# Rows of the first expert by one-hot products on chip, and one looped body for overfull experts

## Chip, cores and metric

One core of one Trainium2 chip runs the whole kernel. The metric is device time in microseconds (us), from launch to end, median over runs. The profile is one execution of its own; the times of its rows count from its first instruction.

## What is computed

A decoder block over 512 tokens of 1024 channels: a token mixer, a layer norm, a mixture of 16 experts (each token goes to 2 of the 4 experts of its best group), and a second layer norm. The change lies at the entry of the mixture.

```python
h = layer_norm(DEEPNORM_ALPHA * h + mix, ln1_g[l], ln1_b[l])
...
group_logits = (t @ router_group_w + router_group_b).astype(f32)
group_p, group_idx = lax.top_k(jax.nn.softmax(group_logits, axis=-1), 1)
...
exp_p, exp_idx = lax.top_k(jax.nn.softmax(in_group, axis=-1), TOP_K_IN_GROUP)
...
h = jax.nn.silu(jnp.einsum("td,edf->tef", t, expert_w_gate)) \
    * jnp.einsum("td,edf->tef", t, expert_w_up)
h = h * combine[:, :, None].astype(h.dtype)
y = jnp.einsum("tef,efd->td", h, expert_w_down)
```

## The kernel before

Tokens lie in four tiles of 128 (`NT` = 4) in `HT`. All large products are three passes on split operands: a high part (written by ScalarE) and a low part (raw minus high, by VectorE); L805 and L809 make the two parts of a piece of expert weights, L1183 and L1184 those of an expert's transposed rows, and L1203, L1204, L1205 multiply high by high, high by low and low by high.

The end of the mixer and the router are one hand-written list of steps (a string, L990 on): `c` and `e` are output projections, `t` transposes, `l` logits, `f` the layer norm of a token tile, `g` the choice of experts, `r` the ranks of the tile's tokens within their experts, and `w8` eight products of ones that use no data (L224). TensorE keeps that order. `choose` writes one-hot rows of the two chosen experts (`EO`, `EA`); `ranks` multiplies `EA` with a triangle (L977), picks each token's rank (L979), and `rank_one_hot` (L929) writes `RO`, a 128 x 128 one-hot matrix of token against rank, for each of a token's two choices.

Behind the list `rank_tokens` (L1024) multiplies `RO` with token numbers, so that column e of `idx` (L1026) lists the 128 rows of expert e. L1034 and L1036 find the largest count, which the program then loads as a branch condition (L1073, L1076): if an expert has more than `CAP` = 128 tokens, a long body treats the others. `gather(e)` (L1042) fetches the rows of expert e from `hD`, a copy of `HT` in device memory (stored at L951), by an indirect DMA that GpSimd issues, into one of five buffers `XG`. The gates (L1054 to L1067) run on VectorE with two exponentials on ScalarE (L1056, L1062); all this stands ahead of the branch. Behind the branch come the low parts of expert 0's weights, tables for the gates and slots (L1137 to L1160), then `turn(0)`: eight transposes of expert 0's rows (L1181) and their two parts, and `gate_up(0, 0)`, its first products. `K` keeps instructions in the order of the program on their engine; the other instructions are put in place by a scheduler. Each engine works through its own list in order.

Of the kernel before, what the change touches and what calls it, by code (L numbers as in the profile page):

```python
# [19 lines left out]
D = 1024  # L20
S = 512
NT = 4
# [14 lines left out]
def body(ctx: ExitStack, tc: tile.TileContext, P: dict, out):  # L37
# [832 lines left out]

    rt = temps(48, 54)
    jp2 = rt(128, dt=I32)
# [19 lines left out]
    EO, EA, rk2 = cst(NT, 2, 16), cst(NT, 16, dt=BF16), cst(NT, 2)  # L892
    TE = late(NT, 2, 2, 16, dt=BF16)
    cmp, ra, rb_, oh2, s16 = rt(5, 4, 4), rt(5, 4), rt(5, 4), rt(2, 5, 4), rt(16)

# [77 lines left out]
    def ranks(i):  # L973

        p = pb()
        for m in range(i + 1):
            K(T.matmul(p[:, 0:16], upper_s if m == i else ones_b, EA[:, m], start=m == 0, stop=m == i))  # L977
        for n in range(2):
            V.scalar_tensor_tensor(s16, EO[:, i, n], 1.0, p[:, 0:16], op0=ALU.mult, op1=ALU.mult,  # L979
                                   accum_out=rk2[:, i, n:n + 1])  # L980
        rank_one_hot(RO, rk2, i)

        V.tensor_scalar(TE[:, i, :, 0], EO[:, i], float(128 * i), None, op0=ALU.mult)
        V.tensor_scalar(TE[:, i, :, 1], EO[:, i], pid, None, op0=ALU.mult)


# [4 lines left out]
    for step in """c0a t00 t10 t01 c0b l00 l10 l01 t11 t20 t30 c1a l11 l20 l30 t02 t03 t21 t31 c1b l02 l03 l21 l31 c2a f0 g0 t12  # L991
                   t13 c2b l12 l13 r0 e0a f1 g1 t22 t23 e0b l22 l23 r1 e1a f2 t32 e1b g2 l32 r2
                   t33 l33 f3 g3 w8 r3""".split():
        kind, v = step[0], [int(x) for x in step[1:3] if x.isdigit()]
        if kind == "c":
            out_half(1, v[0], int(step[2] == "b"))
        elif kind == "e":
            out_half(1, NT - 1, int(step[2] == "b"), slice(v[0] * 256, v[0] * 256 + 256))
        else:
            {"t": transposes, "l": logits_part, "f": finish, "g": choose, "r": ranks, "w": warm}[kind](*v)  # L1000
    eload()
# [14 lines left out]
    rke = cst(NE - NL, NT)  # L1016
    rkv = rke.rearrange("p e i -> p i e")

    def rank_tokens(dst, ro):
# [17 lines left out]

    XG = [reg(o, D) for o in (184, 188, 192, 0, 4)]

    def gather(e):  # L1040
# [4 lines left out]
    earlier = esplit(0, True)  # L1045
    gather(0)
    second = gather(1)
# [22 lines left out]
    yO = dram.tile([(NBLK - 1) * NE * CAP, D], F32, name="yO")  # L1070
    iD = dram.tile([NE * (NBLK - 1), CAP, 1], I32, name="iD")
    with tc.issue_after(second.ins):
# [3 lines left out]
    with tc.If(most > CAP):  # L1076
        OW, OX, OXT, OY = reg(40, 2048), reg(192, D), reg(48, KT, 128), reg(192, D)
        OS, OFT = reg(52, FF), reg(53, FF)
        ORO = reg(48, NT, 2, 128, dt=BF16)
        oidx, ork, oi = cst(NBLK - 1, 16, dt=I32), cst(NT, 2), cst(1, dt=I32)  # L1080
        V.tensor_scalar(gto, rk2, float(CAP), None, op0=ALU.is_ge)
        V.tensor_tensor(gto, gt, gto, ALU.mult)
        for b in range(1, NBLK):
            V.tensor_scalar(ork, rk2, float(CAP * b), None, op0=ALU.subtract)
            for i in range(NT):
                rank_one_hot(ORO, ork, i)
            rank_tokens(oidx[:, b - 1], ORO)
            SP.dma_start(iD.rearrange("(e b) p o -> p b (e o)", b=NBLK - 1)[:, b - 1], oidx[:, b - 1])
        with tc.For_i(0, NE, 1) as eo:
            wex = lambda nm, r: P[nm][0][bass.ds(eo, 1)].rearrange("o (k p) f -> p (o k) f", p=128)[:, r]  # L1090
            for b in range(1, NBLK):
                SP.dma_start(oi, iD[bass.ds(eo * (NBLK - 1) + (b - 1), 1)].rearrange("b p o -> p (b o)"))
                G.indirect_dma_start(out=OX, out_offset=None, in_=hD,
# [23 lines left out]
                for n in range(2):  # L1117
# [4 lines left out]
                    V.tensor_copy(OY[:, ns], p)  # L1122
                SP.dma_start(yO[bass.ds(eo * ((NBLK - 1) * CAP) + (b - 1) * CAP, CAP)], OY)
        osl, oslf = cst(NT, 2, dt=I32), cst(NT, 2)
# [305 lines left out]
```

## Time and profile before

| | |
|---|---|
| three runs | 828.6, 829.49, 836.26 us, median 829.49 |
| profiled execution, its own time | 829.64 us |
| its span, first to last instruction | 827.9 us |
| busy: TensorE, VectorE, ScalarE, GpSimd | 94%, 65%, 46%, 13% |
| mean granted clock of TensorE | 0.976 |

A row of a timeline gives start and busy time of an instruction (or of a run of like ones, xN), engine, line, operation, output <- inputs, and in brackets how long the engine was idle before it and what ended that. PE is TensorE, DVE VectorE, ACT ScalarE, POOL GpSimd; a q behind the name is the engine's sequencer. PEclk is the granted clock of TensorE, 1.00 being 2.4 GHz and 0.50 being 1.2 GHz.

### The profile page before, as it was taken

What the parts mean: (1) busy time and instruction counts of PE and PEld (TensorE: products, weight loads), DVE (VectorE), ACT (ScalarE), POOL (GpSimd) and SP (SyncE); (2) the same over time, 40 slices, a digit from 0 to 9 for tenths busy, and PEclk for the clock granted to TensorE, in tenths of its full rate; (3) what the DMA queues carried; (4) which work ended last, traced back from release to release, by engine and by line L of the source; (5) the groups of instructions that cost most, each with busy time, mean ns of one, the idle gap of its engine ahead of it and who ended that gap; (6) DMA issues with size and microseconds to landing.
All of it is one profiled execution on the core that took longest, in us unless ns stands there. A gap on an engine that the chain in (4) does not pass through costs nothing.

```text
span 827.9 us, 10853 instructions
## 1 busy us (share of the span) xinstructions
PE 779.1 (94%) x4043; PEld 647.5 (78%) x4043; DVE 535.5 (65%) x1026; ACT 385.0 (46%) x612; POOL 106.7 (13%) x90
## 2 busy tenths in 40 slices
PE   8879999999999999999999999999994999999991
PEld 7567888787889988888788888888773788888780
DVE  3337882997575992547633332323578899999987
ACT  2485353453335542423322222222323899899843
POOL 0002002001100000000500000001031202110177
PEclk9998999999999999999999999999996999999996
DMA  9526336336260135343244333369818899999762
GB/s 225 87 59 169 79 81 143 84 69 154 46 139 2 51 72 95 94 102 77 99 129 103 103 101 103 102 241 331 291 52 260 297 382 388 367 341 307 280 250 101
DMA packets 110752, 133.65 MB, mean 161 GB/s; under 512 B 19780, under 2 KB 93032, under 8 KB 110696
## 3 DMA queue, kind: packets, MB, share of 16 engines
q1 hardware_dynamic: 107240, 120.33, 50.2%
q0 software_dynamic: 3456, 12.58, 4.3%
q8 instruction: 33, 0.54, 0.3%
q14 instruction: 23, 0.19, 0.1%
HBM read 120.82 MB, written 12.08 MB: 161 GB/s over the span
## 4 chain that ended last, share of the span: by engine, by line
PE 76%; issue 9%; DVE 9%; DMA 2%; ACT 2%; POOL 1%; POOLq 0%; DVEq 0%; SPq 0%; ACTq 0%
PE pa L237 16%; PE pa L236 16%; PE pa L235 16%; PE pa L1205 5%; PE pa L1203 4%; PE pa L1204 4%; PE pb L1181 2%; PE pb L525 1%; DVE r L809 1%; DVE r L386 1%; PE pb L607 1%; PE pb L592 1%; PE pb L509 1%; DMA r<-hD,r 1%; PE pb L414 1%
## 5 line engine op out<-in xcount | busy, mean ns | idle before, releaser
L235 PE MATMUL pa<-r,r 128*128 128x512 f32 (+1 forms) x712 | 280.1, 393 | 7.5 <-ACT r L149 7.3
L236 PE MATMUL pa<-r,r 128*128 128x512 f32 (+1 forms) x712 | 278.3, 391 | 2.2 <-DVE r L150 2.2
L237 PE MATMUL pa<-r,r 128*128 128x512 f32 (+1 forms) x712 | 277.5, 390 | 0.0
L150 DVE TENSOR_TENSOR r<-r,r 128x2048 fp32r<-128x2048 f32 (+2 forms) x48 | 102.8, 2148 | 134.6 <-ACT r L149 134.6
L235 PEld LDWEIGHTS pa<-r,r 128*128 128x128 f32 x712 | 134.4, 189 | 35.6 <-ACT r L149 8.1
L236 PEld LDWEIGHTS pa<-r,r 128*128 128x128 f32 x712 | 134.5, 189 | 29.5 <-DVE r L150 3.2
L237 PEld LDWEIGHTS pa<-r,r 128*128 128x128 f32 x712 | 134.3, 189 | 27.3 <-DVE r L232 0.4
L149 ACT ACTIVATE r<-r 128x2048 fp32r<-128x2048 f32 (+2 forms) x48 | 84.8, 1777 | 143.3 <-PE pa L236 82.0
L809 DVE TENSOR_TENSOR r<-r,r 128x1024 fp32r<-128x1024 f32 x96 | 117.1, 1222 | 5.6 <-ACT r L805 3.9
L805 ACT ACTIVATE r<-r 128x1024 fp32r<-128x1024 f32 x96 | 96.3, 1059 | 0.0
L1203 PE MATMUL pa<-r,r 128*128 128x512 f32 x192 | 78.2, 407 | 0.0
L1205 PE MATMUL pa<-r,r 128*128 128x512 f32 x192 | 75.9, 395 | 1.0 <-DVE r L1305 1.0
L1204 PE MATMUL pa<-r,r 128*128 128x512 f32 x192 | 75.6, 394 | 0.0
L386 DVE SCALAR_TENSOR_TENSOR r<-pa,r,r 128x511 f32<-128x511 f32 (+2 forms) x72 | 53.5, 743 | 15.7 <-ACT r L384 15.2
L1205 PEld LDWEIGHTS pa<-r,r 128*128 128x128 f32 x192 | 36.0, 188 | 9.9 <-DVE r L1305 1.9
L1203 PEld LDWEIGHTS pa<-r,r 128*128 128x128 f32 x192 | 36.3, 189 | 7.1 <-ACT r L1183 0.2
L1204 PEld LDWEIGHTS pa<-r,r 128*128 128x128 f32 x192 | 36.3, 189 | 6.9
L387 ACT ACTIVATE r<-r 128x512 f32<-128x512 f32 x24 | 15.1, 630 | 46.7 <-DVE r L386 42.9
L1042 POOL DMA_INDIRECT r<-hD,r x16 | 21.1, 1317 | 91.4 <-PE pb L1181 37.3
L758 POOL TENSOR_TENSOR r<-r,r 128x512 f32<-128x512 f32 x8 | 10.3, 1290 | 146.2 <-DVE r L757 142.0
L384 ACT ACTIVATE r<-pa,r 128x512 f32<-128x512 f32 x24 | 16.3, 680 | 25.2 <-PE pa L237 25.2
L1181 PE MATMUL pb<-r,r 128*128 128x128 f32 x128 | 20.2, 284 | 8.3 <-DMA r<-hD,r 8.2
(325 smaller groups left out, 899.0 us busy)
## 6 DMA issues: line engine op xcount, KB each, us to landing
r<-in_w_in_dram SPq DMA_DIRECT2D x29, 1024.0 KB, 8.9
r<-in_expert_w_gate_dram SPq DMA_DIRECT2D x32, 512.0 KB, 6.8
r<-in_expert_w_down_dram SPq DMA_DIRECT2D x16, 1024.0 KB, 8.4
r<-in_expert_w_up_dram SPq DMA_DIRECT2D x32, 512.0 KB, 8.4
yD<-r SPq DMA_DIRECT2D x12, 512.0 KB, 9.7
r<-in_x_dram SPq DMA_DIRECT2D x8, 512.0 KB, 5.9
r<-in_w_dn_out_dram SPq DMA_DIRECT2D x4, 1024.0 KB, 5.5
r<-in_w_sgu_out_dram SPq DMA_DIRECT2D x4, 1024.0 KB, 6.0
```

The source lines that it names most:

```text
L149: pin(A.activation(hi, raw, AF.Copy))
L150: pin(eng.tensor_tensor(lo, raw, f_(hi), ALU.subtract))
L235: pin(T.matmul(o, lh, rh, start=first, stop=False))
L236: pin(T.matmul(o, lh, rl, start=False, stop=False))
L237: pin(T.matmul(o, ll, rh, start=False, stop=last))
L386: V.scalar_tensor_tensor(acc[:, s:], p[:, :S - s], wc(3 - s), acc[:, s:], op0=ALU.mult, op1=ALU.add)
L805: K(A.activation(hi[:, s], raw[:, s], AF.Copy))
L809: K(V.tensor_tensor(lo[:, s], raw[:, s], f_(hi[:, s]), ALU.subtract))
L1181: K(T.transpose(p[:, u * 128:(u + 1) * 128], XG[e % 5][:, k * 128:(k + 1) * 128], ident))
L1203: K(T.matmul(args[0], args[1], args[3], start=args[5], stop=False))
L1204: K(T.matmul(args[0], args[1], args[4], start=False, stop=False))
L1205: K(T.matmul(args[0], args[2], args[3], start=False, stop=args[6]))
```

## The change

Expert 0's rows are no longer gathered. For each token tile VectorE makes `OH0`, a float matrix of token against rank that is one where the token is expert 0's (two instructions, L984 and L985 of the changed kernel). A new step `d` multiplies it with the tile of `HT` (L997, two products of 128 x 512, summed over the four tiles in two PSUM banks); d0 to d2 take the place of `w8`, d3 stands behind r3. ScalarE copies one half of the sum to `XG[0]` (L1033), VectorE the other (L1034). `gather(0)` goes. The code for overfull experts becomes one body in nested loops over blocks and experts instead of three copies; its index table is laid out by block.

```diff
-    rt = temps(48, 54)
+    rt = temps(48, 52)
...
+    OH0 = reg(52, NT, 128)
...
         rank_one_hot(RO, rk2, i)
 
+        V.tensor_scalar(OH0[:, i], RO[:, i, 0], EO[:, i, 0, 0:1], None, op0=ALU.mult)
+        V.scalar_tensor_tensor(OH0[:, i], RO[:, i, 1], EO[:, i, 1, 0:1], OH0[:, i], op0=ALU.mult, op1=ALU.add)
+
...
+    p0 = []
+
+    def dispatch(i):
+
+        for n in range(2):
+            if i == 0:
+                p0.append(pa())
+            K(T.matmul(p0[n], OH0[:, i], HT[:, i, n * 512:(n + 1) * 512], start=i == 0, stop=i == NT - 1))
...
-                   t33 l33 f3 g3 w8 r3""".split():
+                   t33 l33 f3 g3 d0 d1 d2 r3 d3""".split():
...
+
+    XG = [reg(o, D) for o in (184, 188, 192, 0, 4)]
+    K(A.activation(XG[0][:, 0:512], p0[0], AF.Copy))
+    K(V.tensor_copy(XG[0][:, 512:D], p0[1]))
...
-    gather(0)
     second = gather(1)
...
-        for b in range(1, NBLK):
-            V.tensor_scalar(ork, rk2, float(CAP * b), None, op0=ALU.subtract)
+        V.tensor_copy(ork, rk2)
+        with tc.For_i(0, NBLK - 1, 1) as bo:
+            V.tensor_scalar(ork, ork, float(CAP), None, op0=ALU.subtract)
...
-            for b in range(1, NBLK):
-                SP.dma_start(oi, iD[bass.ds(eo * (NBLK - 1) + (b - 1), 1)].rearrange("b p o -> p (b o)"))
+            with tc.For_i(0, NBLK - 1, 1) as bo:
+                SP.dma_start(oi, iD[bass.ds(bo * NE + eo, 1)].rearrange("b p o -> p (b o)"))
```

What TensorE's list holds between the last layer norm (L935 before, L936 in the changed kernel) and the lists of rows. Before: eight products of ones, then the ranks of tile 3 (L977).

```order
L935 MATMUL pb<-r_65,r_4250 128x20
L224 MATMUL pb<-r_110 128x128 x8
L977 LDWEIGHTS r_4256
L977 MATMUL pb<-r_4279,r_4256 128x16
...
L977 LDWEIGHTS r_4254
L977 MATMUL pb<-r_4279,r_4254 128x16
L1031 LDWEIGHTS r_4256
```

In the changed kernel (L978 are the ranks, L1048 the counts; r_3152 is HT, r_4282 is OH0):

```order
L936 MATMUL pb<-r_65,r_4250 128x20
L997 MATMUL pa<-r_3152,r_4282 128x512 x6
L978 LDWEIGHTS r_4256
L978 MATMUL pb<-r_4279,r_4256 128x16
...
L978 LDWEIGHTS r_4254
L978 MATMUL pb<-r_4279,r_4254 128x16
L997 MATMUL pa<-r_3152,r_4282 128x512 x2
L1048 LDWEIGHTS r_4256
```

Six products of 512 columns now stand ahead of the ranks of tile 3 and two behind them, ahead of the counts.

ScalarE's list at the same place, from tile 3's square root (L938, L939 in the changed kernel) to the branch. L805 are the high parts of expert 0's first weights, L1056 and L1062 (L1070 and L1076) the exponentials of the gates. Before:

```order
L938 ACTIVATE r_4271<-r_2948,r_4269 128x1
L805 ACTIVATE r_4714<-r_4203 128x1024 x2
L1056 ACT_TABLE_LOAD
L1056 ACTIVATE r_4720<-r_4720 128x16
L1062 ACTIVATE r_4724<-r_4724 128x4
L1073 TENSOR_LOAD r_4707
L1076 COMPARE_AND_BRANCH
```

In the changed kernel, where pa is d's sum and r_4692 is XG[0]:

```order
L939 ACTIVATE r_4271<-r_2948,r_4269 128x1
L915 ACTIVATE r_4276<-pb 128x256
L926 ACTIVATE r_4250<-pa 20x128
L1033 ACTIVATE r_4692<-pa 128x512
L805 ACTIVATE r_4726<-r_4203 128x1024 x2
L1070 ACT_TABLE_LOAD
L1070 ACTIVATE r_4731<-r_4731 128x16
L1076 ACTIVATE r_4735<-r_4735 128x4
L1087 TENSOR_LOAD r_4724
L1090 COMPARE_AND_BRANCH
```

The copy of half the rows now stands ahead of the weights' high parts and of the table load.

VectorE's list of the changed kernel behind the ranks of tile 3 (L980 is the second pick of a rank, L930 RO, L984 and L985 OH0, L1034 the copy, L1043 the list of rows, L1051 and L1053 the largest count):

```order
L980 SCALAR_TENSOR_TENSOR r_4287,r_4280<-r_4278,pb 128x16
L930 TENSOR_SCALAR r_4277<-r_4259,r_4280 128x128 x2
L984 TENSOR_SCALAR r_4282<-r_4277,r_4278 128x128
L985 SCALAR_TENSOR_TENSOR r_4282<-r_4277,r_4278,r_4282 128x128
L1034 COPY r_4692<-pa 128x512
L1043 CAST r_4689<-pb 128x16
L1051 TENSOR_REDUCE r_4722<-pb 128x1
L1053 CAST r_4724<-r_4722 128x1
L1068 TENSOR_REDUCE r_4733<-r_4249 128x4
```

Before, L929 was followed at once by L1034 and L1036 (the largest count), L1026 (the list) and L1054 (the first step of the gates); what follows in both, to the branch and behind it, is the same list.

## Rows read from the trace of the kernel before

**Rows 1.** The page: TensorE's busy time and that of its weight loads, VectorE and ScalarE with their shares, and TensorE's busy tenths in 40 slices.

```profile
PE 779.1 (94%) x4043; PEld 647.5 (78%) x4043; DVE 535.5 (65%) x1026; ACT 385.0 (46%) x612; POOL 106.7 (13%) x90
...
PE   8879999999999999999999999999994999999991
```

**Rows 2.** Windows: length, then busy us (and count) of PE, PEld, DVE, ACT, POOL, then granted clock, DMA share and GB/s.

```profile
610.00:620.00 10.00, 9.41 (x72) 7.91 (x71) 9.49 (x41) 2.64 (x7) 3.19 (x3) 1.00 0.14 55
620.00:625.00 5.00, 2.53 (x19) 1.70 (x17) 4.84 (x15) 0.16 (x1) 2.74 (x2) 0.90 0.55 164
...
675.00:680.00 5.00, 5.00 (x26) 4.08 (x25) 4.97 (x6) 4.29 (x7) 0.00 (x0) 1.00 1.03 403
```

**Rows 3.** The chain that ended last, in order of time, between the router and expert 0: start, length, engine and line.

```profile
632.78 0.17 DVE r L1026
...
633.82 6.96 DMA r<-hD,r
```

**Rows 4.** TensorE's timeline.

```profile
627.15 3.78 PE L224 MATMUL pb<-r 128*128 128x128 f32 x16
...
630.73 0.27 PE L977 MATMUL pb<-r,r 128*128 128x16 bf16 x3
631.44 0.17 PE L977 MATMUL pb<-r,r 128*128 128x16 bf16 x1 [0.45 <-DVE r L969]
...
632.37 0.37 PE L1024 MATMUL pb<-r,r 128*128 128x16 bf16 x4 [0.36 <-DVE r L929]
640.98 1.94 PE L1181 MATMUL pb<-r,r 128*128 128x128 f32 x8 [8.23 <-DMA r<-hD,r]
...
644.68 0.47 PE L1205 MATMUL pa<-r,r 128*128 128x512 f32 x1
...
658.50 0.50 PE L1205 MATMUL pa<-r,r 128*128 128x512 f32 x1 [0.65 <-DVE r L1305]
```

**Rows 5.** VectorE's timeline.

```profile
619.75 0.24 DVE L956 SCALAR_TENSOR_TENSOR r<-pb,r,r 128x20 f32<-128x20 f32 x1 [0.46 <-PE pb L911]
...
631.21 0.17 DVE L969 TENSOR_TENSOR r<-r 128x16 bf16<-128x16 f32 x1
...
632.06 0.41 DVE L929 TENSOR_SCALAR r<-r,r 128x128 bf16<-128x128 bf16 x2
632.39 0.17 DVE L1034 TENSOR_REDUCE r<-pb 128x1 f32<-128x16 f32 x1
...
632.95 0.28 DVE L1059 TENSOR_TENSOR r<-r,r 128x128 f32<-128x128 f32 x1
...
634.19 0.16 DVE L1057 TENSOR_REDUCE r<-r 128x4 f32<-128x16 f32 x1
...
635.07 0.17 DVE L1065 TENSOR_TENSOR r<-r,r 128x4 f32<-128x4 f32 x1
636.40 0.06 DVE L1137 MEMSET r<- 128x1 f32 x1 [1.17 <-DVEq L1076]
...
642.77 1.50 DVE L1184 TENSOR_TENSOR r<-pb,r 128x512 fp32r<-128x512 f32 x2
```

**Rows 6.** The line with a plain float product of 512 columns: its instructions (shortest, median, longest in ns; first and last start), and TensorE's timeline around it.

```profile
L672 PE MATMUL pb<-r,r x4: 592/592/697, 377.7 to 379.1; 128*128 128x512 f32 x4
...
377.66 1.99 PE L672 MATMUL pb<-r,r 128*128 128x512 f32 x4
...
379.71 0.40 PE L237 MATMUL pa<-r,r 128*128 128x512 f32 x1
379.95 0.40 PE L235 MATMUL pa<-r,r 128*128 128x512 f32 x1
```

**Rows 7.** Windows of one us around the wait for the gather, columns as in rows 2.

```profile
627.00:628.00 1.00, 1.00 (x5) 0.96 (x6) 0.84 (x6) 1.00 (x3) 0.00 (x0) 0.50 1.09 381
...
630.00:631.00 1.00, 0.99 (x8) 0.86 (x7) 0.88 (x5) 0.26 (x1) 0.00 (x0) 0.59 0.97 373
...
634.00:635.00 1.00, 0.00 (x0) 0.00 (x0) 0.83 (x5) 0.47 (x1) 0.95 (x1) 0.61 0.95 370
...
644.00:645.00 1.00, 1.00 (x14) 0.96 (x12) 0.27 (x1) 1.00 (x2) 0.61 (x1) 0.77 0.26 87
```

**Rows 8.** An earlier wait of TensorE: its timeline where work starts again, and the window in which the granted clock rises.

```profile
62.04 0.80 PE L235 MATMUL pa<-r,r 128*128 128x512 f32 x1 [4.53 <-ACT r L149]
...
67.00:68.00 1.00, 1.00 (x7) 0.96 (x7) 1.00 (x2) 0.00 (x0) 0.00 (x0) 0.69 1.16 327
```

**Rows 9.** ScalarE's timeline.

```profile
626.97 1.99 ACT L805 ACTIVATE r<-r 128x1024 fp32r<-128x1024 f32 x2
628.98 1.28 ACT L1056 ACT_TABLE_LOAD   x1
633.35 0.21 ACT L1056 ACTIVATE r<-r 128x16 f32<-128x16 f32 x1 [3.09 <-DVE r L1055]
...
642.10 0.60 ACT L1183 ACTIVATE r<-pb 128x512 fp32r<-128x512 f32 x1 [3.68 <-PE pb L1181]
```

**Rows 10.** ScalarE's timeline at a table load between two activations, early in the span.

```profile
39.66 1.28 ACT L273 ACT_TABLE_LOAD   x1
40.95 0.60 ACT L273 ACTIVATE r<-pa 128x512 f32<-128x512 f32 x1
```

**Rows 11.** GpSimd's timeline: the issue of expert 0's gather.

```profile
633.82 1.14 POOL L1042 DMA_INDIRECT r<-hD,r  x1 [10.99 <-DVE r L1061]
```

More of the change, by code (lines that the diff above doesn't have):

```diff
@@ L999, in body @@
         else:
-            {"t": transposes, "l": logits_part, "f": finish, "g": choose, "r": ranks, "w": warm}[kind](*v)
+            {"t": transposes, "l": logits_part, "f": finish, "g": choose, "r": ranks, "d": dispatch}[kind](*v)
     eload()
@@ L1036, in body @@
     rks = V.tensor_copy(cmi, cmx)
-    XG = [reg(o, D) for o in (184, 188, 192, 0, 4)]
     def gather(e):
@@ L1070, in body @@
     yO = dram.tile([(NBLK - 1) * NE * CAP, D], F32, name="yO")
-    iD = dram.tile([NE * (NBLK - 1), CAP, 1], I32, name="iD")
+    iD = dram.tile([(NBLK - 1) * NE, CAP, 1], I32, name="iD")
     with tc.issue_after(second.ins):
@@ L1079, in body @@
         ORO = reg(48, NT, 2, 128, dt=BF16)
-        oidx, ork, oi = cst(NBLK - 1, 16, dt=I32), cst(NT, 2), cst(1, dt=I32)
+        oidx, ork, oi = cst(16, dt=I32), cst(NT, 2), cst(1, dt=I32)
         V.tensor_scalar(gto, rk2, float(CAP), None, op0=ALU.is_ge)
         V.tensor_tensor(gto, gt, gto, ALU.mult)
-        for b in range(1, NBLK):
-            V.tensor_scalar(ork, rk2, float(CAP * b), None, op0=ALU.subtract)
+        V.tensor_copy(ork, rk2)
+        with tc.For_i(0, NBLK - 1, 1) as bo:
+            V.tensor_scalar(ork, ork, float(CAP), None, op0=ALU.subtract)
             for i in range(NT):
                 rank_one_hot(ORO, ork, i)
-            rank_tokens(oidx[:, b - 1], ORO)
-            SP.dma_start(iD.rearrange("(e b) p o -> p b (e o)", b=NBLK - 1)[:, b - 1], oidx[:, b - 1])
+            rank_tokens(oidx, ORO)
+            SP.dma_start(iD[bass.ds(bo * NE, NE)].rearrange("e p o -> p (e o)"), oidx)
         with tc.For_i(0, NE, 1) as eo:
             wex = lambda nm, r: P[nm][0][bass.ds(eo, 1)].rearrange("o (k p) f -> p (o k) f", p=128)[:, r]
-            for b in range(1, NBLK):
-                SP.dma_start(oi, iD[bass.ds(eo * (NBLK - 1) + (b - 1), 1)].rearrange("b p o -> p (b o)"))
+            with tc.For_i(0, NBLK - 1, 1) as bo:
+                SP.dma_start(oi, iD[bass.ds(bo * NE + eo, 1)].rearrange("b p o -> p (b o)"))
                 G.indirect_dma_start(out=OX, out_offset=None, in_=hD,
@@ L1122, in body @@
                     V.tensor_copy(OY[:, ns], p)
-                SP.dma_start(yO[bass.ds(eo * ((NBLK - 1) * CAP) + (b - 1) * CAP, CAP)], OY)
+                SP.dma_start(yO[bass.ds(eo * ((NBLK - 1) * CAP) + bo * CAP, CAP)], OY)
         osl, oslf = cst(NT, 2, dt=I32), cst(NT, 2)
```

## The prediction

> **What bounds the kernel now.** I read the page first, then the windows, then the chain, then each engine's timeline around the one place where TensorE stops. TensorE is busy 94% of the span, and one of the 40 slices stands out [rows 1]. In the expert stage (675 to 680 us) TensorE is busy in every microsecond, and VectorE and ScalarE nearly so [rows 2], so whatever delays its entry stays in the time. Between the router and expert 0 the chain goes: last ranks on TensorE, index list on VectorE (L1026), gather of expert 0's rows at 633.82 with 6.96 us to landing [rows 3], and eight transposes at 640.98, for which TensorE has sat idle 8.23 us [rows 4]. This is what the change removes.
>
> The reader should then look at what VectorE does in those 8.23 us. From the end of the gates (L1065, 635.07) it passes the branch on the overfull experts (L1137 at 636.40, after 1.17 us), computes the low parts of expert 0's weights and some tables without a pause, and reaches the low part of expert 0's transposed rows (L1184) at 642.77, two pieces in 1.50 us [rows 5]. TensorE's first product that needs the first piece (ready at 643.52) is L1205 at 644.68 [rows 4]. So two queues arrive almost together: gather to transposes, and gates to branch to low parts, the second with 1.16 us to spare. If the gather vanished and nothing else moved, about 1.1 us would be gained, not 8.2.
>
> **The change, step by step.** Times are on the axis of the profiled execution before, which took 829.64 us (span 827.9 and 1.74 around it; the median of three runs is 829.49, so the sum speaks for both).
>
> *One-hot matrices on VectorE.* Each token tile adds two instructions of 128 x 128 float (L984, L985 of the change). The trace has no such pair; the nearest are L929 (two of 128 x 128 in 0.41 us) and L1059 (0.28 us by itself) [rows 5]. I take 0.45 us a pair; the bounds are 0.3 and 0.55. The pairs of tiles 0 to 2 fall where VectorE is busy 9.49 of 10 us and 4.84 of 5 [rows 2], where it holds the chain to TensorE up; the one pause there that I found is 0.46 us at L956 [rows 5]. Three pairs are 1.35, less 0.46: **+0.9 us** (0 to 1.35). The stretch in which TensorE now warms (L224 at 627.15) therefore begins at 628.05.
>
> *d0, d1, d2 instead of w8.* Six products of 128 x 512 in plain float. L672 is the one line with that shape: the program has two, the trace shows four instructions of 592 ns and more, which overlap. They run from 377.66 to the start of L237 at 379.71, less 0.24 us for the one L236 between (the pace from L237 to the L235 behind it): 1.81 us, so 0.45 an instruction and 0.91 a product at granted clock 1.00 [rows 6]. At half clock I take the warm-up's own pace: 16 instructions of 128 columns from 627.15 to 630.73 [rows 4] are 0.224 each; four times that is 0.895 for 512 columns and 1.79 a product. Which level holds? The granted clock is 0.50 at 627, rises late in the slice 630 to 631 (its mean is 0.59), that is 3.7 us after the warm-up began, and has fallen again by 635 [rows 7]. A second rise has TensorE busy from 62.04 and the clock up at about 67.7, 5.6 us later [rows 8]. With 3.7 us at half clock 2.07 products are done and 3.93 are left at 0.91: 7.3 us in all. With 5.6 us it is 8.2; at full clock throughout it would be 5.46. I take **7.7 us**, end at 635.75. The last ranks (r3) are queued behind; the choice that they need was done at 631.38 (L969 [rows 5]), 632.3 with the 0.9, so this is a new wait of over 3 us. Before, the last r3 matmul started at 631.44 [rows 4]; now it does at 635.85.
>
> *d3.* From that matmul to the last one-hot rows took VectorE 0.93 us (L1024 starts again at 632.37 [rows 4]); tile 3's pair adds 0.45, the hop 0.05: d3 starts at 637.28. Four instructions of 0.45 and 0.14 for the rest of the last one (592 ns): the sums are in PSUM at **639.2**. Whether the clock stays up over TensorE's 1.4 us pause I leave to the range; at half clock d3 costs 1.75 more.
>
> *The copy, and who stands behind it on ScalarE.* This is the step that the diff does not show. In before ScalarE does the high parts of expert 0's first weights (L805, 1.99 us) at 626.97 and loads the exponential table at 628.98, long before they are wanted [rows 9]. In the changed order the copy of half the rows (L1033) stands ahead of both, and it waits for d3. So from 639.2 ScalarE does the copy (0.60, as L1183), the L805 pair (1.99), the table (1.28) and the first exponential (0.21) [rows 9]: about 643.3. VectorE's sum over that exponential (L1057, at 634.19 [rows 5]) cannot start before. VectorE alone would get there at about 641.8 (its own copy 0.75, as one piece of L1184, then 1.80 for the list, the maximum and the gates, as from L1034 at 632.39 to L1057 [rows 5]), so ScalarE's queue is the later: **643.35, that is 9.15 us late**.
>
> The Trainium skill, ScalarE: Activation LUTs, section What ACT_TABLE_LOAD costs, gives a switch of tables 1283 ns and a drain of about 1380 ns on top, 2.66 us in all. The trace shows the load alone: it starts at 39.66, takes 1.28, and the next activation starts at 40.95 [rows 10]. By the page the sum would be 1.4 us larger; I go by the rows.
>
> *Behind the branch.* The branch (1.17 us) and VectorE's queue after it keep their order and length: 636.40 becomes 645.55, and the first low part of expert 0's rows, done at 643.52 before, becomes 652.65. TensorE, which needed it at 644.68, now waits for it: **+8.0 us**. The transposes are no longer the last to arrive: the rows are on chip by 639.9, and the transposes can start at about 645.6.
>
> *The clock at the entry.* In before the clock was up from 644.5 [rows 7]. Now TensorE is mostly idle from about 640 to 652, so I count its restart at half clock for 3.5 to 5.6 us, of which half is lost, 1.75 to 2.8, and take back the 0.65 us at 658.50 for which it waited on VectorE [rows 4]: **+1.6 us** (0 to 2.2).
>
> *What costs nothing.* One gather less: issuing it took GpSimd 1.14 us [rows 11], and nothing waits for GpSimd there. Expert 1's gather now needs the list at about 640.5, is issued 0.9 us behind it, as expert 0's was, and with the same 6.96 us lands at 648.4, before 652.65; that cover is some 4 us. The weight loads behind the branch on SyncE shift with it, as do the buffers that they wait for. The overfull experts' code isn't executed (no record of it), so its loops are worth only what jumping over it costs: VectorE's 1.17 us at the branch. A shorter body could save some of it; VectorE's own part of the body is hardly shorter, so I take 0 (bound: 0.6 us gained).
>
> **Sum:** +8.0 and +1.6 is +9.6; 829.64 + 9.6 = **839.2 us**.
>
> **Rivals.**
> 1. *The clock is kind.* All six products at full clock (5.46 instead of 7.7, so 2.2 less) and no loss at the restart (1.6 less): +5.8, **835.4 us**. For it: once up, the clock stays up through steady work. Against it: it was at 0.50 when the warm-up began [rows 7]. If the three early pairs hide as well, 834.5.
> 2. *The clock is unkind.* d3 at half clock (+1.75), 8.2 for the first six (+0.5), restart at its upper bound (+0.6): +12.4, **842.0 us**. For it: the clock fell after the short stretch of work before 634 [rows 7].
> 3. *Not slower: VectorE and ScalarE have room after all.* If the gather alone held TensorE, the transposes would start when the copies are done, at 639.9 instead of 640.98, and the time would be **828.5 us**. It decides if VectorE's work behind the branch can start by 636.4 as now, which needs the rank sums before d0 to d2, or the gates before the copy. The printed order speaks against both. More than 1% faster (below 821.2) would take nearly the whole 8.23 us wait at no price at all.
> 4. *The loops do it.* If the jump over the long body stalls instruction fetch in before, the change would win up to 0.6 us by the only gap that the trace shows there; it decides neither sign.
>
> **Numbers.** My forecast (the sum, 837 to 841) has 0.46, rival 1 0.24, rival 2 0.22, rival 3 0.05; 0.03 stay for a gain by something that I don't see. 1% of this time, about what a measurement of this kernel can tell from no change, is 8.3 us, so slower begins at 837.8. The forecast's lower edge (0.02) and rivals 1 and 3 lie within it: 0.31 the same; 0.66 slower; 0.03 faster. The range runs from rival 1's lower edge, 834.5, to just above rival 2, 843, and leaves out rival 3, the unseen gain and the tails, under 2 in 10.
>
> **What would show it.** In the changed kernel: L997 in two groups, the first some 7 to 8 us long with part of it at granted clock 0.50, and r3's matmuls behind it; ScalarE idle from about 628 to 639, then L1033, L805 and the table load in a row; VectorE waiting on ScalarE before the sum of the exponentials; the transposes ending their wait on VectorE's branch, not on a DMA; and TensorE's longest wait in that stretch now ended by L1199 on VectorE. The prediction is wrong if r3 is done by 633, if the exponential is done before the copies, or if TensorE's first full group of expert 0 starts before 648. It is also wrong if a wait that the order does not show, for instance a late weight load or the second gather, ends last.

## The result: 838.05 us, one per cent slower

Over 20 runs of each kernel the changed one takes 838.05 us in the median (835.07 to 841.51), the one before 829.75 us (824.54 to 838.16). The ratio is 1.0100 with a 95% interval of 1.0084 to 1.0115, so the change costs 7.0 to 9.5 us. The forecast was 839.2 us.

The profiled execution of the changed kernel took 835.32 us (span 833.6), near the lower end of its 20 runs; that of before, 829.64 us, is at its median. So the two traces differ by 5.7 us where the medians differ by 8.3, and what the trace shows has to be completed by a second execution of the same work (experiment 2).

Executions also reach the changed stretch at different times, since TensorE's waits at the program's start vary (those for ScalarE's L149 add up to 6.2 to 7.3 us in five of the traces). I therefore count from a mark A that stands in every trace: the start of VectorE's first long 128 x 80 instruction in the choice of experts of tile 2 (L961 before, L962 after). It is at 620.02 before and at 619.60 after.

```profile
620.02 1.29 DVE L961 TENSOR_TENSOR r<-r 128x80 f32<-128x80 f32 x1
```

```profile
619.60 1.38 DVE L962 TENSOR_TENSOR r<-r 128x80 f32<-128x80 f32 x1
```

A hides one thing: the new one-hot pairs of tiles 0 and 1 run on VectorE ahead of it. A mark ahead of all pairs, B, is the first 128 x 80 instruction in the choice of experts of tile 0 (L961 before, then L962 after):

```profile
607.99 0.24 DVE L961 TENSOR_TENSOR r<-r 128x80 f32<-128x80 f32 x1
```

```profile
607.10 0.24 DVE L962 TENSOR_TENSOR r<-r 128x80 f32<-128x80 f32 x1
```

From B to A it is 12.03 us before and 12.50 after; over the fourteen traces used below it is 12.02 to 12.03 in the five without the pairs and 12.49 to 12.51 in the nine with them. So wherever a kernel with the products is set against one without them, it is 0.47 us later than times behind A show.

### The profile page after: what moved, and what is told of

Its sections match the earlier page's. It is cut to its first block, busy times and chain, and to the rows that moved or that the text cites. A ratio compares the mean times of both kernels' runs of the same rounds, so it can differ in the third digit from the quotient of the medians.

```text
span 833.6 us, 10869 instructions
## 1 busy us (share of the span) xinstructions
PE 785.4 (94%) x4043; PEld 648.0 (78%) x4043; DVE 537.3 (64%) x1035; ACT 384.6 (46%) x613; POOL 106.0 (13%) x89
## 5 line engine op out<-in xcount | busy, mean ns | idle before, releaser
L149 ACT ACTIVATE r<-r 128x2048 fp32r<-128x2048 f32 (+2 forms) x48 | 84.7, 1776 | 141.0 <-PE pa L236 84.2
L805 ACT ACTIVATE r<-r 128x1024 fp32r<-128x1024 f32 x96 | 96.4, 1060 | 0.0
L1218 PE MATMUL pa<-r,r 128*128 128x512 f32 x192 | 79.0, 411 | 0.6 <-ACT r L1198 0.6
L1220 PE MATMUL pa<-r,r 128*128 128x512 f32 x192 | 76.5, 399 | 1.2 <-DVE r L1320 0.9
L1219 PE MATMUL pa<-r,r 128*128 128x512 f32 x192 | 75.8, 395 | 0.0
L1220 PEld LDWEIGHTS pa<-r,r 128*128 128x128 f32 x192 | 36.5, 190 | 10.7 <-DVE r L1320 1.8
L1218 PEld LDWEIGHTS pa<-r,r 128*128 128x128 f32 x192 | 36.7, 191 | 7.7 <-ACT r L1198 1.0
L1219 PEld LDWEIGHTS pa<-r,r 128*128 128x128 f32 x192 | 36.8, 192 | 7.0
L1057 POOL DMA_INDIRECT r<-hD,r x15 | 19.1, 1271 | 100.2 <-PE pb L1196 37.0
L758 POOL TENSOR_TENSOR r<-r,r 128x512 f32<-128x512 f32 x8 | 12.5, 1558 | 142.7 <-DVE r L757 136.0
L1198 ACT ACTIVATE r<-pb 128x512 fp32r<-128x512 f32 x32 | 19.0, 595 | 17.1 <-PE pb L1196 9.9
```

The lines of the kernel that those rows point to most:

```text
L149: pin(A.activation(hi, raw, AF.Copy))
L805: K(A.activation(hi[:, s], raw[:, s], AF.Copy))
L1057: return G.indirect_dma_start(out=XG[e % 5], out_offset=None, in_=hD, in_offset=bass.IndirectOffsetOnAxis(ap=idx[:, e:e + 1], axis=0))
L1218: K(T.matmul(args[0], args[1], args[3], start=args[5], stop=False))
L1219: K(T.matmul(args[0], args[1], args[4], start=False, stop=False))
L1220: K(T.matmul(args[0], args[2], args[3], start=False, stop=args[6]))
```

## The profile after

The page of the changed kernel, busy times and TensorE's tenths, against [rows 1]: TensorE has 6.3 us more, and the one thin slice (4) has become three (7, 6, 8).

```profile
PE 785.4 (94%) x4043; PEld 648.0 (78%) x4043; DVE 537.3 (64%) x1035; ACT 384.6 (46%) x613; POOL 106.0 (13%) x89
...
PE   8889999999999999999999999999976899999991
```

TensorE's timeline of the changed kernel, where [rows 4] stood: d0 to d2 (L997 x12), the ranks r3 (L978), d3 (L997 x4), counts and lists, transposes (L1196), products of high by high and high by low (L1218, L1219), low by high (L1220).

```profile
626.37 6.90 PE L997 MATMUL pa<-r,r 128*128 128x512 f32 x12
633.10 0.25 PE L978 MATMUL pb<-r,r 128*128 128x16 bf16 x4
634.87 1.98 PE L997 MATMUL pa<-r,r 128*128 128x512 f32 x4 [1.51 <-DVE r L985]
...
636.79 0.55 PE L1041 MATMUL pb<-r,r 128*128 128x16 bf16 x16
642.33 1.94 PE L1196 MATMUL pb<-r,r 128*128 128x128 f32 x8 [4.99 <-DVEq L1090]
...
648.21 1.10 PE L1196 MATMUL pb<-r,r 128*128 128x128 f32 x4
649.64 0.80 PE L1220 MATMUL pa<-r,r 128*128 128x512 f32 x1 [0.34 <-DVE r L1199]
```

The reader should see three things. The ranks stand behind d0 to d2. The transposes no longer wait for a DMA: the branch on VectorE's sequencer (DVEq) ends their wait. And the first product on a low part waits for VectorE's L1199, at 649.64 instead of 644.68.

VectorE's timeline of the changed kernel, against [rows 5]: choice of tile 3 done (L972), second wait for the ranks (L980), the one-hot pair (L984, L985), the copy (L1034), the sum over the exponential (L1071), the branch (L1152), the low parts of expert 0's rows (L1199).

```profile
631.20 0.17 DVE L972 TENSOR_TENSOR r<-r,r 128x16 f32<-128x16 bf16 x1
633.40 0.17 DVE L980 SCALAR_TENSOR_TENSOR r<-r,pb 128x16 f32<-128x16 f32 x1 [2.03 <-PE pb L978]
...
634.14 0.28 DVE L984 TENSOR_SCALAR r<-r,r 128x128 f32<-128x128 bf16 x1
634.46 0.35 DVE L985 SCALAR_TENSOR_TENSOR r<-r,r,r 128x128 f32<-128x128 bf16 x1
636.96 0.69 DVE L1034 COPY r<-pa 128x512 f32<-128x512 f32 x1 [2.15 <-PE pa L997]
...
640.12 0.17 DVE L1071 TENSOR_REDUCE r<-r 128x4 f32<-128x16 f32 x1 [0.81 <-ACT r L1070]
...
642.34 0.06 DVE L1152 MEMSET r<- 128x1 f32 x1 [1.17 <-DVEq L1090]
...
648.91 1.27 DVE L1199 TENSOR_TENSOR r<-pb,r 128x512 fp32r<-128x512 f32 x2
```

Three waits are new here: 2.03 us for the ranks, 2.15 for d3, 0.81 for ScalarE. In the kernel before VectorE has only the wait at the branch (1.17 us) in the same work, and the changed kernel has that one too. ScalarE's timeline of the changed kernel, against [rows 9], shows why VectorE waits for it: the copy (L1033) waits for d3's first half, and the weights' high parts and the table load come behind it.

```profile
636.08 0.60 ACT L1033 ACTIVATE r<-pa 128x512 f32<-128x512 f32 x1 [9.98 <-PE pa L997]
636.57 1.99 ACT L805 ACTIVATE r<-r 128x1024 fp32r<-128x1024 f32 x2
638.58 1.28 ACT L1070 ACT_TABLE_LOAD   x1
639.87 0.21 ACT L1070 ACTIVATE r<-r 128x16 f32<-128x16 f32 x1
```

Windows of the changed kernel (columns as in [rows 2], the granted clock third from the end): half clock from 626 to about 629.4, up until 639.6, half again until about 653.3.

```profile
626.00:627.00 1.00, 0.85 (x2) 0.68 (x3) 0.96 (x4) 0.09 (x1) 0.00 (x0) 0.50 1.03 368
...
629.00:630.00 1.00, 1.00 (x3) 0.53 (x2) 0.79 (x5) 0.00 (x0) 0.00 (x0) 0.81 0.27 108
...
639.00:640.00 1.00, 0.00 (x0) 0.00 (x0) 0.28 (x1) 0.99 (x3) 0.71 (x1) 0.81 0.10 25
...
653.00:654.00 1.00, 1.00 (x5) 0.77 (x5) 0.00 (x0) 0.31 (x1) 0.00 (x0) 0.86 0.07 25
```

## Experiments

Each row is the profiled execution of one kernel, in us behind its A: start of the last matmul of the ranks of tile 3 (where all four run together, of the first of them, 0.08 to 0.13 us earlier), of the gates' sum over the exponential, of VectorE behind the branch, of TensorE's first product on a low part of expert 0's rows, and the end of the span. The kernel before and 1, 3, 8 and 10 have no pairs ahead of A; against them every other row is 0.47 us later than its numbers say. The last column is the ratio of medians to the kernel before on the same chip, with its 95% interval.

| kernel | ranks | gates | branch | low part | end | ratio |
|---|---|---|---|---|---|---|
| before | 11.42 | 14.17 | 16.38 | 24.66 | 207.88 | 1 |
| changed | 13.50 | 20.52 | 22.74 | 30.04 | 214.00 | 1.0100 (1.0084 to 1.0115) |
| 1 loops only | 11.27 | 14.01 | 16.22 | 23.84 | 207.18 | 0.9995 (0.9966 to 1.0023) |
| 2 rows only | 15.10 | 22.12 | 24.35 | 31.49 | 215.49 | 1.0102 (1.0067 to 1.0137) |
| 3 no gather | 11.39 | 14.14 | 16.36 | 23.45 | 207.38 | 1.0016 (0.9992 to 1.0040) |
| 4 spread | 12.86 | 19.84 | 22.07 | 29.37 | 214.78 | 1.0092 (1.0058 to 1.0126) |
| 5 d3 behind | 15.05 | 18.13 | 20.34 | 27.43 | 211.23 | 1.0070 (1.0045 to 1.0094) |
| 6 late | 11.25 | 14.14 | 16.36 | 26.24 | 209.78 | 1.0054 (1.0032 to 1.0077) |
| 7 late, low first | 11.11 | 14.00 | 16.22 | 25.14 | 209.09 | 1.0072 (1.0045 to 1.0099) |
| 8 before, low first | 11.41 | 14.16 | 16.37 | 22.32 | 207.00 | 1.0002 (0.9982 to 1.0022) |
| 9 copy behind | 13.65 | 19.79 | 22.00 | 29.10 | 214.78 | 1.0080 (1.0050 to 1.0109) |
| 10 no gather, low first | 11.41 | 14.16 | 16.38 | 21.79 | 206.76 | 0.9983 (0.9956 to 1.0011) |
| 11 filler | 14.92 | 21.93 | 24.18 | 31.27 | 216.87 | 1.0091 (1.0058 to 1.0124) |
| 12 late halves | 11.11 | 14.00 | 16.21 | 21.50 | 206.36 | 1.0018 (0.9998 to 1.0037) |

The theory is the forecast's: d0 to d2 hold up the ranks, and d3, the copy and ScalarE's queue hold up the gates; VectorE's queue behind the branch passes that on to the first low part. The rivals: the loops cost something; the gather alone held TensorE; the products cost their own time wherever they stand.

**1 and 2, the change in two halves.** Loops only is the kernel before with the looped body; rows only is the kernel before with this and nothing else:

```diff
+    OH0 = reg(52, NT, 128)
...
-                   t33 l33 f3 g3 w8 r3""".split():
+                   t33 l33 f3 g3 d0 d1 d2 r3 d3""".split():
...
+    K(A.activation(XG[0][:, 0:512], p0[0], AF.Copy))
+    K(V.tensor_copy(XG[0][:, 512:D], p0[1]))
...
-    gather(0)
```

> The kernel before with one half of the change: the code for overfull experts as one body in loops, the rows of expert 0 still gathered. Theory (all of the loss is in the one-hot products and in what they hold up): 829.2 to 830.5 us, ratio 0.999 to 1.001, gates at the time they have in the kernel before. Rival (the jump over the body, or the register work of the loops, costs something on every engine): 831 to 838 us, with longer stretches at the branch on TensorE and VectorE.

> The kernel before with the other half: the rows of expert 0 by one-hot products, the code for overfull experts still unrolled. Theory: as the whole change, 837 to 839 us, ratio 1.009 to 1.011. Rival (the loops bear a part of the loss): 830 to 836 us. If this one is slower than the whole change, the loops gave something back.

Measured: 829.44 us against 829.25, and 838.72 against 829.25. All of the loss is in the rows; the loops bring and cost nothing that shows, and the gap at the branch stays at 1.17 us. The second trace also shows the same work in another draw of the clock. TensorE's timeline of rows only (L1001 are d0 to d3):

```profile
627.39 8.48 PE L1001 MATMUL pa<-r,r 128*128 128x512 f32 x12
635.71 0.25 PE L978 MATMUL pb<-r,r 128*128 128x16 bf16 x4
```

Its granted clock rises late (below, at 633), and d0 to d2 hold TensorE for 8.32 us up to r3 (635.71 less 627.39) instead of 6.73.

```profile
627.00:628.00 1.00, 0.83 (x2) 0.68 (x3) 0.98 (x3) 0.11 (x1) 0.00 (x0) 0.50 1.06 372
...
633.00:634.00 1.00, 1.00 (x3) 0.24 (x3) 0.00 (x0) 0.00 (x0) 0.00 (x0) 0.70 1.32 348
```

Its end is 7.6 us behind that of before, by A, where the other trace of the same order has 6.1; by B it is 8.1 and 6.6.

**3, 8 and 10, the two queues.** What would the gather's removal be worth by itself? No gather lets expert 0 read the rows of token tile 0 (that part of the computation is left out), low first moves the second weights piece behind the low parts of the rows, on VectorE's queue; 10 has both.

```diff
-    gather(0)
...
-            K(T.transpose(p[:, u * 128:(u + 1) * 128], XG[e % 5][:, k * 128:(k + 1) * 128], ident))
+            K(T.transpose(p[:, u * 128:(u + 1) * 128], (XG[e % 5] if e else HT[:, 0])[:, k * 128:(k + 1) * 128], ident))
```

```diff
-    later()
     turn(0, 0)
     turn(0, 1)
+    later()
```

> The kernel before without the gather of expert 0's rows and with nothing in its place; left out: expert 0 gets the rows of the first token tile. Theory (two queues end together there, the gather's and the one that runs from the gates over VectorE's branch to the low parts): the gain is only 0.5 to 2 us, 828 to 829.3 us. Rival (the gather alone holds TensorE up): 5 to 8 us less, 822 to 825 us.

> Control: the kernel before with that move of the second piece alone, the gather kept. Theory (the gather holds the transposes at 641 us, so a shorter queue on VectorE gains little): 828.8 to 830 us, ratio 0.999 to 1.001. Rival (VectorE's queue alone held TensorE up): 826.5 to 828 us.

> The kernel before without the gather of expert 0's rows (left out: expert 0 gets the rows of the first token tile) and with the second weights piece split behind the low parts of the rows. Neither half alone moved the time. Theory (gather and VectorE's queue are two paths that end together): with both gone the first low part comes 1.5 to 2.5 us earlier, 826.5 to 828.5 us. Rival (something behind both, such as the loads of the next weights, sets the time): 829 to 830.5 us, and the low part's head start is lost later.

Measured: 830.45 against 829.25; 829.22 against 829.60; 828.26 against 830.20. The rival, 5 to 8 us by the gather alone, falls; the half to two us that the theory gave experiment 3 do not show in its median either. In the trace the first low part comes 1.2 us earlier without the gather (the forecast said some 1.1), and the end 0.5; but in the trace of loops only, with the gather in place, they come 0.8 and 0.7 us earlier, so one execution doesn't tell this gain from none. With both it comes 2.9 us earlier, the end 1.1; the interval of the ratio still holds 1. In 8 and 10 that product also stands ahead of four transposes and eight small products (L1275, L1274 in 10) that precede it in the kernel before, so the next piece is the better mark. There the clock has taken a part: in experiment 10 TensorE starts on expert 0 at 19.00 behind A instead of 20.96, but the granted clock rises at 24.1 behind A, against 24.4 before (slice means 0.72 at 646 to 647 and 0.77 at 644 to 645), so what starts earlier runs at half clock, and at the transposes of the next piece only 1.15 us of the head start are left (28.63 against 29.78). So nearly nothing was to be had at this place, whatever the rows cost.

One step of mine was too sharp here. In experiment 8 the gather is still there, yet the transposes start at 19.52 behind A (639.02) and not at 20.96:

```profile
639.02 1.94 PE L1181 MATMUL pb<-r,r 128*128 128x128 f32 x8 [6.81 <-DVE r L1152]
```

There the wait ends with one of VectorE's table steps (L1152), so the rows were on chip before: they landed at most 5.7 us after GpSimd began to issue the gather (633.29), against 7.0 in [rows 3]; in loops only it is 6.3 (632.66 to 638.99). The gather's duration varies by more than the 1.16 us between the two queues, so which of them ends last changes from execution to execution.

**4, the products spread.** Only the list of steps differs from the changed kernel.

```diff
-                   t13 c2b l12 l13 r0 e0a f1 g1 t22 t23 e0b l22 l23 r1 e1a f2 t32 e1b g2 l32 r2
-                   t33 l33 f3 g3 d0 d1 d2 r3 d3""".split():
+                   t13 c2b l12 l13 r0 e0a f1 g1 t22 t23 e0b l22 l23 r1 e1a f2 t32 e1b g2 l32 d0 d1 r2
+                   t33 l33 f3 g3 d2 r3 d3""".split():
```

> The changed kernel with another order of its steps alone: the products of token tiles 0 and 1 stand in TensorE's pause ahead of the ranks of tile 2, those of tile 2 where the filler products stood, those of tile 3 unchanged. Theory (the loss comes from the products of tiles 0 to 2 that stand ahead of the ranks of tile 3): the ranks, the gates and the first low part come some 3 us earlier than in the changed kernel, 834 to 836 us. Rival (the loss comes from the copies of the rows and ScalarE's queue, or from the products wherever they stand): 837 to 839 us, first low part not earlier.

Measured: 838.10 us, the theory's number missed. TensorE's timeline of this kernel:

```profile
623.23 3.70 PE L997 MATMUL pa<-r,r 128*128 128x512 f32 x8
626.77 0.22 PE L978 MATMUL pb<-r,r 128*128 128x16 bf16 x3
...
631.38 3.40 PE L997 MATMUL pa<-r,r 128*128 128x512 f32 x4 [2.38 <-DVE r L957]
```

d0 and d1 vanish in the pause as meant: r2's matmuls stand at 5.05 behind A, where the last of them starts at 4.60 in the changed kernel (624.20). But d2 alone now stands for 2.38 us, since on VectorE the second half of tile 2's one-hot pair (630.90 for 0.34) stands behind two full-width instructions of the layer norm, and it then runs at half clock, four instructions in 3.40 us. The ranks come 0.6 to 2.2 us earlier than in the two traces of the changed order, not 3, and r3 to gates keeps its full 7.0 us. So the products' place matters by what they wait for too, and the larger part of the loss lies behind r3.

**5 and 9, what stands between ranks and gates.** In 5 d3 goes behind counts and lists, and both copies go to ScalarE behind the exponentials. In 9 the copy on ScalarE moves behind the weights' high parts (the pair L805, which the expectation calls low parts), and VectorE's copy behind counts and lists in the program; on VectorE it now follows the largest count, not the other way round. In both an ordering hint (`issue_after`) keeps L805 behind the last logits.

```diff
-                   t33 l33 f3 g3 d0 d1 d2 r3 d3""".split():
+                   t33 l33 f3 g3 d0 d1 d2 r3""".split():
...
-    K(A.activation(XG[0][:, 0:512], p0[0], AF.Copy))
-    K(V.tensor_copy(XG[0][:, 512:D], p0[1]))
...
-    earlier = esplit(0, True)
+    dispatch(3)
+    with tc.issue_after(lgs[NT - 1].ins):
+        earlier = esplit(0, True)
...
+    with tc.issue_after(rks.ins):
+        K(A.activation(XG[0][:, 0:512], p0[0], AF.Copy))
+        K(A.activation(XG[0][:, 512:D], p0[1], AF.Copy))
```

```diff
-    K(A.activation(XG[0][:, 0:512], p0[0], AF.Copy))
-    K(V.tensor_copy(XG[0][:, 512:D], p0[1]))
...
-    earlier = esplit(0, True)
+    K(V.tensor_copy(XG[0][:, 512:D], p0[1]))
+    with tc.issue_after(lgs[NT - 1].ins):
+        earlier = esplit(0, True)
+    K(A.activation(XG[0][:, 0:512], p0[0], AF.Copy))
```

> The changed kernel with the product of token tile 3 behind the counts and the lists, and both copies of expert 0's rows on ScalarE behind the gates' exponentials; the products of tiles 0 to 2 stay ahead of the ranks of tile 3. Theory (from those ranks to the gates the changed kernel loses 4.2 us to the one-hot pair, the wait for the product, the copy and ScalarE's queue; the products of tiles 0 to 2 cost 1.8 us on top): the first gate reduction comes 3.3 to 3.6 us behind the ranks' last product instead of 6.9, the first low part some 3 us earlier, 834 to 836 us. Rival (the time goes with TensorE's work, wherever it stands): 837 to 839 us.

> The changed kernel with one thing moved on ScalarE: the copy of the first half of expert 0's rows stands behind the pair of low-part activations of the first weights piece. Theory (the copy at the head of ScalarE's queue costs only what VectorE waits for the exponential, 0.81 us in the changed kernel's trace; the rest of the loss stays): that wait gone, the pair back in the pause at the time of the kernel before, 836.5 to 838 us. Rival (ScalarE's queue is the larger part of the loss): 833 to 835.5 us.

Measured: 833.91 us against 829.60, and 835.74 against 830.20. In 5 the gates follow the ranks by 3.08 us (18.13 less 15.05), against 7.02 in the changed kernel and 2.75 before: 3.9 of the 4.3 us that the change adds there are gone, though d0 to d2 had the slow draw. Its end lies 4.3 us ahead of rows only, which had the same draw. In 9 the step is 6.14 us, 0.88 less, where 0.81 was forecast. ScalarE's timeline of 9, with L805 back in the pause and the exponential no longer late:

```profile
625.62 1.99 ACT L805 ACTIVATE r<-r 128x1024 fp32r<-128x1024 f32 x2
635.84 0.60 ACT L1061 ACTIVATE r<-pa 128x512 f32<-128x512 f32 x1 [8.23 <-issue]
636.46 1.28 ACT L1071 ACT_TABLE_LOAD   x1
638.17 0.22 ACT L1071 ACTIVATE r<-r 128x16 f32<-128x16 f32 x1 [0.43 <-DVE r L1070]
```

Its first low part is 0.94 us earlier, yet its end gains nothing (214.78): the transposes of the next piece are only 0.3 us earlier (36.54 against 36.85), as the granted clock rises at 34.0 behind A instead of 33.7 (slice means 0.88 and 0.86 at 653 to 654), and the tail behind TensorE's last product is 1.05 us longer (18.35 against 17.30). Its median lies between what the two theories gave, so the whole-run time doesn't decide here; the trace does.

**11, the clock at the restart.** The changed kernel with 16 products of ones (L224) behind the lists.

```diff
+    warm(16)
     earlier = esplit(0, True)
```

> The changed kernel with filler products on TensorE between the lists and the branch, so that it does not stand for 5 us ahead of the first transposes of expert 0. Theory (the restart at half clock costs 1.6 to 1.7 us): the products of expert 0's first piece go at the full clock from the start, first chunk done 1.5 to 2 us earlier, 836 to 837 us. Rival (the clock costs nothing there, since the products wait for weights or low parts anyway): 838 us and the chunk no earlier.

Measured: 837.40 us against 830.20; the theory's head start didn't come. Its windows:

```profile
645.00:646.00 1.00, 0.46 (x5) 0.22 (x2) 1.00 (x3) 1.00 (x2) 0.00 (x0) 1.00 0.00 0
646.00:647.00 1.00, 0.05 (x1) 0.05 (x1) 1.00 (x2) 1.00 (x3) 0.35 (x1) 0.54 0.00 0
...
656.00:657.00 1.00, 1.00 (x5) 0.82 (x4) 0.63 (x1) 1.00 (x2) 0.54 (x1) 0.84 0.00 0
```

The clock stays up through the filler and the transposes, then TensorE waits for ScalarE and VectorE (1.50 and 1.59 us), the clock falls at 646, and the products run at half clock until 656. The fall was only moved. So the size of the restart's loss is not tested by this run; it is read from the trace alone.

**6, 7 and 12, the products out of the way.** d0 and d1 in the pause ahead of r2, w8 back ahead of r3, the one-hot pairs of tiles 2 and 3 on GpSimd, d2 and d3 behind the lists, copies on ScalarE behind the exponentials. 7 adds low first; 12 also does half 0 of tiles 2 and 3 first, copies that on ScalarE ahead of the branch, and half 1 on VectorE behind it, and it moves the second weights piece whole, ScalarE's high parts too.

```diff
+                   t13 c2b l12 l13 r0 e0a f1 g1 t22 t23 e0b l22 l23 r1 e1a f2 t32 e1b g2 l32 d0 d1 r2
+                   t33 l33 f3 g3 w8 r3""".split():
...
+    for i in (2, 3):
+        one_hot(G, i)
+        dispatch(i)
```

```diff
+    for n in range(2):
+        for i in (2, 3):
+            K(T.matmul(p0[n], OH0[:, i], HT[:, i, n * 512:(n + 1) * 512], start=False, stop=i == NT - 1))
...
         earlier()
+        K(V.tensor_copy(XG[0][:, 512:D], p0[1]))
...
-    later()
     turn(0, 0)
     turn(0, 1)
+    esplit(1)
```

> The changed kernel with the products of tiles 0 and 1 in TensorE's pause ahead of the ranks of tile 2, the filler products back ahead of the ranks of tile 3, the one-hot pairs of tiles 2 and 3 on GpSimd, their products behind counts and lists, the copies on ScalarE behind the exponentials. Theory (all of the loss is the place ahead of the gates): ranks and gates at the times of the kernel before, 828.5 to 831 us, ratio 0.999 to 1.002. Rival (the products cost time wherever they stand, by TensorE's time or its clock): 833 to 838 us.

> The same, with the second piece of expert 0's weights split behind the low parts of the rows of expert 0, which shortens VectorE's queue ahead of them by 2.4 us. Theory (gather and gates are two queues that ended together; with both short TensorE starts earlier): 826.5 to 828.5 us, faster than both kernels. Rival (the products or the copies end too late to let the transposes start earlier): 828.5 to 831 us, no gain over the order before.

> Products as in the run with everything late, but first half of the rows of tiles 2 and 3 first and its copy on ScalarE ahead of the branch, the second half's copy on VectorE behind the branch, so that ScalarE loads no table twice; second weights piece behind the low parts. Theory (there, ScalarE's second copy and the two table loads around it held the first low parts up by 3 to 5 us): first low part at or 1 us ahead of the kernel before, 828 to 830.5 us. Rival (the products at half clock behind the lists hold it up): 832 to 835 us.

Measured: 833.36 and 835.34 us against 829.60, and 830.83 against 830.20. The ranks and gates of 6 are within 0.5 us of where they were before (11.25 and 14.14 behind A, 0.3 and 0.4 later by B), so the first part of the theory holds. But its total missed and lies in the rival's range, because the loss had found another place: one copy fell behind the branch. ScalarE's timeline of 6:

```profile
639.97 1.28 ACT L1097 ACT_TABLE_LOAD   x1 [0.41 <-ACTq L1104]
641.27 0.60 ACT L1097 ACTIVATE r<-pa 128x512 f32<-128x512 f32 x1
641.88 1.28 ACT L1163 ACT_TABLE_LOAD   x1
...
643.29 1.98 ACT L805 ACTIVATE r<-r 128x1024 fp32r<-128x1024 f32 x2
```

Two table loads and the copy keep L805 from starting until 643.29, 21.07 behind A, against 16.41 in the kernel before (636.43), and VectorE stands 2.70 us for it. Low first on top (7) didn't cure that: expected 826.5 to 828.5 (its rival 828.5 to 831), measured 835.34. Its profiled execution, 831.17 us, was the fastest of 11, so its trace doesn't show where the median lies. In 12 ScalarE loads one table less behind the branch, TensorE has the first low part 2.7 us ahead of before by B (3.2 by A), and the end is 1.1 us earlier (1.5 by A); the median, just above the theory's range, is 0.2% above before, with 1 just inside the interval. All but 0.6 of the 8.3 us are back, and no version of the change beat the kernel before. Not all of that is the products' place: 12 has low first too, and experiment 8, low first without the products, is its fair neighbour. By B the ends of the two traces lie 0.2 us apart (218.86 and 219.02), and the ratios (1.0018 and 1.0002) differ by less than their intervals. TensorE's timeline of 12 (L1211 transposes, L1235 the first product on a low part):

```profile
634.02 5.40 PE L1071 MATMUL pa<-r,r 128*128 128x512 f32 x8
639.83 0.63 PE L1211 MATMUL pb<-r,r 128*128 128x128 f32 x4 [0.41 <-PEq L1105]
...
643.24 0.50 PE L1235 MATMUL pa<-r,r 128*128 128x512 f32 x1 [0.89 <-DVE r L1214]
```

It still spends 5.40 us on d2 and d3, in the pause in which TensorE used to stand. So the rival that the products cost their time wherever they stand falls.

## Why the prediction was right

Direction, size and mechanism held: the order of the new waits is the one worked out from the printed order. One sign did not come as stated: TensorE's longest wait for VectorE behind the branch is 1.79 us, ended by L1160, a table step of the same queue, and L1199 ends a last wait of only 0.34 us; the queue is the one that was named. By its own steps, with the changed kernel's trace first and rows only, the same order in another execution, second:

- **One-hot pairs, +0.9.** Behind A the choice of tile 3 was done 0.11 us later (L972 at 11.60; L971 before, 631.51, at 11.49), but that is the pair of tile 2 alone. With the 0.47 that A hides the three pairs cost 0.58 us: less than forecast, within its bounds (0 to 1.35).
- **Start of d0, 8.03 behind A.** It was 6.77 and 6.78; by B 19.27 and 19.28 instead of 20.06, so 0.8 us too late in the sum. Besides the pairs, the clock was still up at 625, so the logits ahead of it (L924) took 0.61 us and not 1.04. I had carried over the fall at 624 from before. Why it fell later is open.
- **d0 to d2, 7.7 us.** 6.73 and 8.32; with experiments 9, 11 and 5 (6.94, 7.73, 8.27) the five traces of this order average 7.6. The step was right in the mean, and its spread is that of the clock's rise, 3.0 us behind the start of d0 in one, about 6 in the other. Together with the start: ranks +2.6 and +4.2 us by B (2.1 and 3.7 by A) instead of +4.4. In the profiled execution they start at 633.10, just behind the 633 at which the prediction would have been wrong by its own sign.
- **Ranks to gates, 7.5 us.** 7.02 in both, 4.3 more than before. The order was right. But the copy waits only for the first half of d3, so it began at 636.08, ahead of d3's end (636.85), and ScalarE was 0.8 us earlier than I had it; the one-hot pair took 0.67 instead of 0.45. Experiment 5 shows this step to be the larger part of the loss. The Trainium skill, ScalarE: Activation LUTs, section What ACT_TABLE_LOAD costs, would have added a drain of about 1.4 us. Here the load takes 1.28 us and the exponential starts 0.01 us behind its end (638.58, 639.87), as in [rows 10], so the measurement decides against that.
- **Gates to first low part.** 9.5 and 9.4 us against 9.3 in the forecast. The 1.0 us that the new path takes less than before (10.5) is the slack that the forecast counted as 1.15.
- **Restart at half clock, +1.6.** Too large, within its bounds (0 to 2.2): from the first low part to the end of the span the changed order loses 0.7 and 0.8 us. The sum counted 2.3 lost and 0.65 given back. The transposes of the next piece start 7.1 and 7.8 us later than before by A (656.45 against 649.80 in the first), 1.7 and 0.9 more than the first low part. The 0.65 us did not come back where the sum put it: TensorE still waits 0.48 and 0.64 us there for VectorE. What else was given back is a shorter tail behind TensorE's last product, 17.30 and 17.77 us against 17.95; over the fourteen traces that tail varies from 17.3 to 18.4, so luck has a part in it. Experiment 11 could not separate this term.
- **Nothing for the loops.** Shown by experiment 1.
- **1.1 us for the gather alone.** 1.2 in the trace of experiment 3, but 0.8 in that of experiment 1, which has the gather; nothing in the median. The gather's own duration varies by as much.

So the sum's 9.6 us are 6.6 and 8.1 in two traces by B (6.1 and 7.6 by A) and 8.3 in the medians. Three terms were each 0.5 to 0.9 us too large in both traces: the start of d0, ranks to gates, and the restart. d0 to d2 is 1.0 too large in the first and 0.6 too small in the second. Rival 1's number (835.4) is that of the profiled execution (835.32), but by luck: neither of its conditions held there, since d0 to d2 ran in part at half clock (6.73 us and not 5.46) and TensorE restarted at half clock until 653.3.

## What to carry to other kernels

Before a transfer is replaced by computing, look at which other queue ends just behind it: here about 1 us was all that could be gained, and the new work went ahead of the path that ends there. Place such work by what stands behind it on every in-order engine: a copy that waits at the head of ScalarE's list costs what the table load behind it delays, and the same products in pauses cost next to nothing. When one trace and the medians disagree, compare several traces from a mark inside the program, and put the mark ahead of everything that the change adds.

## What the runs showed of the hardware

- The same six products in the same order took 6.73 to 8.32 us in five executions, by when the granted clock rose from 0.50 to 1.00 within them.
- A copy on ScalarE that was moved behind the branch brought a table load of 1.28 us of its own, and the activation behind it another (experiment 6).
- The one-hot instructions of 128 x 128 took 0.28 and 0.35 us on VectorE and 0.45 to 0.71 on GpSimd, except one: the first of tile 2 took 1.66 to 1.74 in all three executions that have it (L976 of experiment 6 at 630.02 for 1.74, while VectorE ran a 128 x 1024 instruction).
- An earlier restart of TensorE did not bring an earlier rise of the granted clock: in the five executions without the products it started on expert 0 at 18.9 to 21.0 us behind A, and the clock rose from 0.50 to 1.00 at 23.8 to 24.4.
- The indirect gather of 128 rows took at most 5.7, 6.3 and 7.2 us from the start of its issue to the first use of its rows in three executions, for the same list.
